# The w_ada products in rows of 16 matmuls of 128 columns, their loads on GpSimd's queue

## The chip, the cores and the metric

One core of one Trainium2 chip runs the whole program. The metric is the device time of one execution in microseconds (us); the runs of the kernel before are given by their median.

## The reference, cut to what matters

Two layers of a decoder trunk over 256 tokens of width 1024, in float32. Each layer is modulated by six vectors of 1024 numbers (shift, scale and gate of the token mixer and of the channel mixer), which come from one conditioning vector `c` and a weight of 24 MB per layer:

```
c_act = silu(c)
for l in range(2):
    mod = c_act @ w_ada[l] + b_ada[l]            # 1024 -> 6 * 1024
    sh1, sc1, g1, sh2, sc2, g2 = split(mod, 6)
    h = rmsnorm(x, ln1_g[l]) * (1 + sc1) + sh1
    x = x + g1 * mixer(h, ...)                   # GLA branch + RWKV-7 branch, gated merge
    h = rmsnorm(x, ln2_g[l]) * (1 + sc2) + sh2
    f = swiglu(h, ...) if l == 0 else moe(h, ...)   # dense on layer 0, top-2 of 8 experts on layer 1
    x = x + g2 * f
return rmsnorm(x, lnf_g)
```

The change is in `c_act @ w_ada[l]` alone. The product has one row, so it has no natural place on a 128x128 array: it is spread over the rest of the program as filler.

## The kernel before, in words

The program runs through `mixer(k, 0)`, `ffn(k, 0)`, `mixer(k, 1)` and `moe(k, 1)`. All weights are streamed from memory. A float32 weight tile `raw` (128x2048, 1 MB, three buffers) is split into a high and a low part, `hi` by ScalarE (L353) and `lo` by VectorE (L354), and `project` (L367) multiplies it in three matmuls of 256 columns per chunk of 128 rows (L379 to L381). In the feed-forward part each of the 22 passes has 48 of these and 24 more in `second` (L1007 to L1009).

**The w_ada work.** The first two groups of layer 0 (shift and scale of the first mixer) are computed at the start, in `start` (L453), from a repacked copy, already in matmuls of 128 columns. The other ten groups (four of layer 0, six of layer 1) are cut into 8 pieces each, 80 pieces in all; a piece is 128 rows by 1024 columns (512 KB), held in a tile `araw` with `ARAW_BUFS = 4` buffers. `feed` (L238) takes the next piece: `c` is the stationary operand, repeated over 32 columns, and four matmuls of 256 columns write to partitions 0 to 31, 32 to 63, 64 to 95 and 96 to 127 of one PSUM bank, so that they use four separate strips of the array. After the eighth piece of a group two more steps are due, one per later call: ScalarE copies the result (L265), and TensorE transposes it (L270) and VectorE adds the bias (L273). A float32 matmul is recorded as two instructions, so a piece is 8 recorded matmuls.

`pace` (L232) decides when `feed` is called: each projection adds its number of 128-row chunks, and a call is made whenever the sum passes `PACE[phase]`, (10, 22, 15) for the mixer of layer 0, the feed-forward part and the mixer of layer 1. `need` (L280) makes the missing calls at once where a modulation vector is used.

`ahead` (L224), called at the end of each `feed`, issues the load of the next piece on SyncE's queue (L229). With four buffers that load goes into the buffer that the feed just before it has read, so it waits until those matmuls are done.

**What sets the order.** In the mixers and the feed-forward part SyncE's queue runs in the order of the program text (`LOADS`, `manual_schedule`); it carries the `raw` loads (L364) and the `araw` loads alike, and what stands behind a waiting load waits too. The order on TensorE, VectorE, ScalarE and GpSimd is made by the framework's scheduler, which plays the program through with estimated times and gives a free engine the earliest ready instruction; an engine then executes that order as it stands. A w_ada piece whose data is there can so be drawn ahead of its place in the text into a hole on TensorE. In `moe` the order is written out by hand, and the queue streams 352 MB of expert weights.

GpSimd does little: it clears tiles at the start, one piece of `TT` in each mixer (L690), and helps at the start and end of `moe` (L1092, L1423, L1436).

Of the kernel before, what the change touches and what calls it, by code (L numbers as in the profile page):

```python
# [9 lines left out]
F32 = mybir.dt.float32  # L10
# [8 lines left out]
P = 128  # L19
T = 256  # L20
D = 1024
KC = 8
# [135 lines left out]
class K:  # L158
# [65 lines left out]
    def ahead(self):  # L224

        while self.todo and len(self.units) < ARAW_BUFS:
            l, g, kc = self.todo.pop(0)
            w = self.st.tile([P, D], F32, name="araw", bufs=ARAW_BUFS)
            self.nc.sync.dma_start(w, self.A["wada"][l, kc * P:(kc + 1) * P, g * D:(g + 1) * D])  # L229
            self.units.append((l, g, kc, w))  # L230

    def pace(self, n):  # L232
        self.paced += n
        if self.paced >= PACE[self.phase]:
            self.paced -= PACE[self.phase]
            self.feed()

    def feed(self):  # L238


        nc = self.nc
        if self.late:
            return self.late.pop(0)()
        if not self.units:
            self.ahead()
        if not self.units:
            return
        l, g, kc, w = self.units.pop(0)
        if kc == 0:
            self.acc = self.ps.tile([P, 512], F32, name="ada")  # L250
        for j in range(4):
            nc.tensor.matmul(self.acc[32 * j:32 * j + 32, :T], self.c32[:, kc, :], w[:, j * T:(j + 1) * T],  # L252
                             start=kc == 0, stop=kc == KC - 1)
        if kc == KC - 1:
            self.late = self.finish(l, g, self.acc)
        self.ahead()
# [141 lines left out]
MOE_BUFS = 15  # L398
PLACES = [f"raw{i}" for i in range(6)] + ["acts", "late"] + [f"raw{i}" for i in range(6, MOE_BUFS)]
FIRST = ["acts", "late"] + [f"raw{i}" for i in (6, 7, 8, 4, 5, 12, 13, 14, 9, 10, 11, 2, 3, 1, 0)] + ["y"]  # L400
PACE = (10, 22, 15)
ARAW_BUFS = 4
SPLIT_BUFS = 5
R_BUFS = 6
# [1315 lines left out]
```

## Time and profile before

| | us |
|---|---|
| median of 3 runs (lowest, highest) | 1825.53 (1822.11, 1826.31) |
| the profiled execution's own time | 1822.8 |
| its span, first to last instruction | 1821.0 |
| TensorE busy | 1749.7 (96%) |
| VectorE busy | 1090.0 (60%) |
| ScalarE busy | 863.9 (47%) |
| GpSimd busy | 15.8 (1%) |

The span and all rows are of the profiled execution. A busy TensorE is not one at its peak. Times in rows count from the span's start. By the trace `start` and the mixer of layer 0 take the first 390 us, the feed-forward part lasts to 608, the mixer of layer 1 to about 945, and the experts take the rest.

### The profile page before, as it was taken

To read this page: it belongs to the slowest core of one execution; us is meant where nothing else is said; L and a number is where in the kernel's file an instruction comes from. 1 tells how busy PE (TensorE), PEld (TensorE's weight loads), DVE (VectorE), ACT (ScalarE), POOL (GpSimd) and SP (SyncE) were. 2 spreads that over 40 slices of the span, in tenths; PEclk is the share of its full clock that TensorE was granted. 3 is DMA by queue.
4 is the path that set the end of the run, shared out by engine and by line. 5 is a ranking of instruction groups with operands and counts; after the bars stand their busy time and mean duration, and the time that the engine had idled before them with its cause. 6 is when DMAs were issued, how large, how long until landed. Compare 5 with 4: busy or idle time off the path is not lost.

```text
span 1821.0 us, 31549 instructions
## 1 busy us (share of the span) xinstructions
PE 1749.7 (96%) x12447; PEld 1409.9 (77%) x12447; DVE 1090.0 (60%) x1876; ACT 863.9 (47%) x1402; POOL 15.8 (1%) x25
## 2 busy tenths in 40 slices
PE   7998999999999999999979999999999999999997
PEld 7787888989898897789977875578756876578754
DVE  3778355665454679566777972289505983189611
ACT  3743243554343564245546761277405772167501
POOL 0000000000000000000010000000000000000001
PEclk9999899999999899899988999999999999999999
DMA  9624166663735432434595989999999999999995
GB/s 347 261 78 178 42 237 239 259 251 117 296 130 218 162 128 93 163 102 177 170 422 213 349 306 412 421 421 421 416 421 421 420 421 417 421 421 421 420 421 216
DMA packets 79981, 521.03 MB, mean 286 GB/s; under 512 B 9520, under 2 KB 10160, under 8 KB 22352
## 3 DMA queue, kind: packets, MB, share of 16 engines
q1 hardware_dynamic: 78672, 517.04, 71.5%
q8 instruction: 100, 1.64, 0.4%
q10 hardware_dynamic: 1152, 1.89, 0.3%
q14 instruction: 57, 0.47, 0.1%
HBM read 517.84 MB, written 1.05 MB: 285 GB/s over the span
## 4 chain that ended last, share of the span: by engine, by line
PE 87%; DVE 7%; DMA 3%; ACT 1%; issue 1%; SPq 0%; ACTq 0%; DVEq 0%
PE pj L1308 11%; PE pj L379 8%; PE pj L381 8%; PE pj L380 8%; PE pj L1312 6%; PE pj L1313 5%; PE pj L1314 5%; PE pc L1327 5%; PE pc L1330 3%; PE pc L1332 3%; PE pc L1331 3%; DMA raw<-win 2%; PE ada L252 2%; PE pg L1357 1%; DVE lo L354 1%; DVE zt L697 1%
## 5 line engine op out<-in xcount | busy, mean ns | idle before, releaser
L1092 DVE TENSOR_TENSOR lo<-raw,hi 128x1024 fp32r<-128x1024 f32 x330 | 396.0, 1222 | 85.2 <-ACT hi L1091 77.4
L1091 ACT ACTIVATE hi<-raw 128x1024 fp32r<-128x1024 f32 x330 | 347.5, 1059 | 128.2 <-PE pj L1313 80.2
L354 DVE TENSOR_TENSOR lo<-raw,hi 128x512 fp32r<-128x512 f32 x402 | 270.3, 689 | 127.6 <-ACT hi L353 119.9
L353 ACT ACTIVATE hi<-raw 128x512 fp32r<-128x512 f32 x402 | 242.4, 627 | 212.1 <-PE pj L380 126.0
L379 PE MATMUL pj<-hh,hi 128*128 128x256 f32 x1040 | 305.5, 294 | 9.3 <-ACT hi L353 6.9
L381 PE MATMUL pj<-hh,lo 128*128 128x256 f32 x1040 | 301.5, 291 | 3.7 <-DVE lo L354 3.5
L380 PE MATMUL pj<-hl,hi 128*128 128x256 f32 x1040 | 298.3, 288 | 0.1
L379 PEld LDWEIGHTS pj<-hh,hi 128*128 128x128 f32 x1040 | 202.4, 195 | 24.9 <-ACT hi L353 13.5
L381 PEld LDWEIGHTS pj<-hh,lo 128*128 128x128 f32 x1040 | 201.7, 194 | 9.8 <-DVE lo L354 7.8
L380 PEld LDWEIGHTS pj<-hl,hi 128*128 128x128 f32 x1040 | 202.3, 195 | 1.8 <-DVE hl L390 0.8
L1308 PE MATMUL pj<-raw,xs 128*64 128x256 f32 x1792 | 201.3, 381 | 0.0
L1312 PE MATMUL pj<-hi,xh 128*128 128x512 f32 x448 | 181.3, 405 | 0.5 <-ACT hi L1091 0.5
L1314 PE MATMUL pj<-lo,xh 128*128 128x512 f32 x448 | 178.4, 398 | 1.9 <-DVE lo L1092 1.9
L1313 PE MATMUL pj<-hi,xl 128*128 128x512 f32 x448 | 177.6, 397 | 0.0
L1308 PEld LDWEIGHTS pj<-raw,xs 128*64 128x64 f32 x1792 | 125.8, 137 | 64.9 <-issue 4.7
L1352 DVE TENSOR_TENSOR late<-late,pj 128x512 f32<-128x512 f32 (+1 forms) x56 | 30.8, 549 | 207.5 <-PE pj L1308 201.0
L1314 PEld LDWEIGHTS pj<-lo,xh 128*128 128x128 f32 x448 | 84.4, 188 | 25.7 <-DVE lo L1092 5.3
L1327 PE MATMUL pc<-raw,as 128*64 128x512 f32 x448 | 102.2, 595 | 0.0
L1312 PEld LDWEIGHTS pj<-hi,xh 128*128 128x128 f32 x448 | 84.6, 189 | 21.4 <-ACT hi L1091 2.0
L1313 PEld LDWEIGHTS pj<-hi,xl 128*128 128x128 f32 x448 | 84.7, 189 | 18.8
L1330 PE MATMUL pc<-hi,acts 128*128 128x512 f32 x224 | 88.2, 394 | 0.0
L1332 PE MATMUL pc<-lo,acts 128*128 128x512 f32 x224 | 87.5, 391 | 0.0
(404 smaller groups left out, 2586.6 us busy)
## 6 DMA issues: line engine op xcount, KB each, us to landing
raw<-moe SPq DMA_DIRECT2D x333, 1024.0 KB, 18.6
raw<-win SPq DMA_DIRECT2D x43, 1024.0 KB, 6.1
araw<-wada SPq DMA_DIRECT2D x80, 512.0 KB, 6.0
raw<-f SPq DMA_DIRECT2D x33, 1024.0 KB, 8.2
raw<-wv SPq DMA_DIRECT2D x8, 1024.0 KB, 5.8
raw<-wog SPq DMA_DIRECT2D x8, 1024.0 KB, 5.8
raw<-wad SPq DMA_DIRECT2D x6, 1024.0 KB, 7.3
raw<-wor SPq DMA_DIRECT2D x4, 1024.0 KB, 5.0
```

Of the source, the lines that this page charges most:

```text
L353: nc.scalar.activation(hi[:, :w], src, AF.Copy)
L354: nc.vector.tensor_tensor(lo[:, :w], src, hi[:, :w].bitcast(F32), ALU.subtract)
L379: nc.tensor.matmul(o, hi[:, s], ah[:, kc, :], start=kc == 0, stop=False)
L380: nc.tensor.matmul(o, hi[:, s], al[:, kc, :], start=False, stop=False)
L381: nc.tensor.matmul(o, lo[:, s], ah[:, kc, :], start=False, stop=kc == nk - 1)
L1091: nc.scalar.activation(hi, w[:, s], AF.Copy)
L1092: eng.tensor_tensor(lo, w[:, s], hi.bitcast(F32), ALU.subtract)
L1308: nc.tensor.matmul(p[64 * n:64 * n + 64, :T], x[:, kc], hi[:, z * 512 + n * T:z * 512 + n * T + T], start=kc == 0, stop=kc == KC - 1)
L1312: nc.tensor.matmul(p, x[0][:, kc], hi[:, s], start=kc == 0, stop=False)
L1313: nc.tensor.matmul(p, x[1][:, kc], hi[:, s], start=False, stop=False)
L1314: nc.tensor.matmul(p, x[0][:, kc], lo[:, s], start=False, stop=kc == KC - 1)
L1327: nc.tensor.matmul(py[0][64 * n:64 * n + 64], act[:, a:a + CAP], hi[:, s], start=first, stop=last)
```

## The change: what it does

A call of `feed` takes two pieces instead of one and issues each as eight matmuls of 128 columns instead of four of 256, so 16 matmuls (32 recorded) stand together. `PACE` is changed to (18, 36, 26), which calls `feed` about half as often. The loads of the pieces are issued on GpSimd's queue instead of SyncE's. Number of pieces, of buffers and of bytes stay as they are.

```diff
@@ ahead
-            self.nc.sync.dma_start(w, self.A["wada"][l, kc * P:(kc + 1) * P, g * D:(g + 1) * D])
+            self.nc.gpsimd.dma_start(w, self.A["wada"][l, kc * P:(kc + 1) * P, g * D:(g + 1) * D])
@@ feed
-        l, g, kc, w = self.units.pop(0)
-        if kc == 0:
-            self.acc = self.ps.tile([P, 512], F32, name="ada")
-        for j in range(4):
-            nc.tensor.matmul(self.acc[32 * j:32 * j + 32, :T], self.c32[:, kc, :], w[:, j * T:(j + 1) * T],
-                             start=kc == 0, stop=kc == KC - 1)
+        for _ in range(2):
+            l, g, kc, w = self.units.pop(0)
+            if kc == 0:
+                self.acc = self.ps.tile([P, 512], F32, name="ada")
+            for h in range(2):
+                for j in range(4):
+                    nc.tensor.matmul(self.acc[32 * j:32 * j + 32, h * P:(h + 1) * P], self.c32[:, kc, :],
+                                     w[:, j * T + h * P:j * T + (h + 1) * P], start=kc == 0 and h == 0,
+                                     stop=kc == KC - 1, skip_group_check=True)
         if kc == KC - 1:
             self.late = self.finish(l, g, self.acc)
         self.ahead()
@@ constants
-PACE = (10, 22, 15)
+PACE = (18, 36, 26)
```

## Rows read from the trace of the kernel before

**Rows 1.** The page: span, and busy time of each engine.
```profile
span 1821.0 us, 31549 instructions
PE 1749.7 (96%) x12447; PEld 1409.9 (77%) x12447; DVE 1090.0 (60%) x1876; ACT 863.9 (47%) x1402; POOL 15.8 (1%) x25
```

**Rows 2.** Window of the experts' stage: PE, PEld, DVE, ACT, POOL busy; clock, DMA, GB/s.
```profile
980.00:1821.00 841.00, 824.59 (x4712) 580.33 (x4712) 479.25 (x546) 412.17 (x514) 5.09 (x11) 1.00 0.97 396
```

**Rows 3.** Waits of SyncE's queue: waiter, releaser, total us, times, longest.
```profile
SPq L229 <- PE ada L252: 460.5, 45, 50.2
```

**Rows 4.** Timeline of SyncE's queue: start of the first load, us to the second's end.
```profile
460.84 9.72 SPq L229 DMA_DIRECT2D araw<-wada  x2
```

**Rows 5.** The chain that ended last, in order of time: start us, us, what.
```profile
302.95 14.27 DMA raw<-win
...
470.66 5.92 DMA raw<-f
...
579.10 5.80 DMA raw<-f
```

**Rows 6.** Windows of the feed-forward part: columns as in the experts' row.
```profile
487.63:496.27 8.64, 8.64 (x75) 8.64 (x73) 4.92 (x9) 4.43 (x8) 0.00 (x0) 1.00 0.96 398
469.53:477.34 7.81, 3.71 (x44) 1.43 (x43) 0.19 (x2) 1.07 (x3) 0.00 (x0) 0.77 0.76 284
477.34:487.63 10.29, 10.29 (x73) 10.07 (x73) 7.24 (x12) 5.83 (x11) 0.00 (x0) 0.85 1.01 419
577.98:585.66 7.68, 3.28 (x43) 1.19 (x42) 0.41 (x3) 1.06 (x3) 0.00 (x0) 0.82 0.79 297
585.66:596.34 10.68, 10.68 (x72) 10.46 (x73) 5.80 (x10) 5.20 (x11) 0.00 (x0) 0.81 1.02 420
390.35:607.86 217.51, 208.87 (x1732) 198.33 (x1733) 112.24 (x196) 100.01 (x188) 0.00 (x0) 0.97 0.55 212
```

**Rows 7.** Timeline of TensorE around three bursts: start us, us, what, xcount.
```profile
533.59 0.28 PE L381 MATMUL pj<-hh,lo 128*128 128x256 f32 x1
533.80 0.64 PE L252 MATMUL ada<-araw,c 128*32 128x256 f32 x8
534.37 0.38 PE L379 MATMUL pj<-hh,hi 128*128 128x256 f32 x1
...
61.57 1.93 PE L252 MATMUL ada<-araw,c 128*32 128x256 f32 x32
...
29.08 0.28 PE L476 MATMUL pj<-hh,lo 128*128 128x256 f32 x1
29.29 1.96 PE L453 MATMUL ada<-raw,c 128*32 128x128 f32 x64
31.18 0.38 PE L473 MATMUL pj<-hh,hi 128*128 128x256 f32 x1
```

**Rows 8.** Windows of line L252 alone: stretch, its length, PE and PEld busy.
```profile
130.00:220.00 90.00, 6.33 (x64) 1.67 (x56) 0.89 0.31 113
...
300.00:390.35 90.35, 10.48 (x142) 3.70 (x131) 1.00 0.66 247
390.35:607.86 217.51, 12.40 (x144) 3.98 (x144) 0.97 0.55 212
...
sum 818.00, PE 56.68 PEld 17.69; mean PE 9.45 PEld 2.95
```

**Rows 9.** Timeline of TensorE in the tail of the first mixer.
```profile
318.01 0.39 PE L379 MATMUL pj<-hh,hi 128*128 128x256 f32 x1 [2.74 <-ACT hi L353]
```

**Rows 10.** Instructions on tile araw: TensorE idle until its loads landed; time to landing.
```profile
  DMA araw<-wada: 8.5, 4
...
DMA to landing us min/median/max: 3.6/6.0/15.6
```

**Rows 11.** Timeline of GpSimd: start us, us, what, idle before and releaser.
```profile
376.98 0.95 POOL L690 MEMSET TT<- 32x1024 f32 x1 [340.54 <-DVE lo L354]
```

## The prediction

> **What bounds the kernel now.** I read the page first, then stages. TensorE is busy 96% of the span and no other engine over 60% [rows 1]; the program is bound by TensorE and by how fast weights reach it. The experts' stage is bound by transfers: the DMA engines are busy 97% of 841 us [rows 2]. It has no w_ada work and its stream begins when the mixer before it gives its buffers back, so what is gained before it moves it forward whole, and nothing is gained inside it. The question is what happens before that stage.
>
> The waits of SyncE's queue give the first answer. In 45 places the queue stood, 460.5 us in all and up to 50.2 us at once, because a w_ada load (L229) waited for the matmuls (L252) that read its buffer [rows 3]. The `raw` loads behind it stand too. Mostly that is covered by three `raw` buffers. In the feed-forward part it is not: a w_ada load issued at 460.84 is followed by another whose issue ends 9.72 us later [rows 4], and only then, at 470.66, comes the next `raw` load, on which the chain that ended last lies for 5.92 us; at 579.10 the same again for 5.80 us [rows 5]. These are the two pile-ups that the reader should see in the windows. A clean pass takes 8.64 us with 72 weight matmuls, 0.12 each. From 469.53 TensorE is busy 3.71 of 7.81 us, and the next pass takes 10.29; from 577.98 it is busy 3.28 of 7.68, and the next takes 10.68 [rows 6]. The longer passes show a granted clock of 0.85 and 0.81: the clock fell to its lower level (1.2 of 2.4 GHz) for part of them, after TensorE had stood half idle. In the holes the scheduler put five w_ada pieces each, ahead of their places, and these too had to wait for their loads.
>
> **The matmuls: rows of 128 columns.** From the matmul before a lone piece to the one after it are 534.37 - 533.59 = 0.78 us; less the ordinary step of 0.12 a piece displaces 0.66 us. Four pieces in one burst last 1.93 us against 0.64 for one [rows 7], so a further piece costs (1.93 - 0.64) / 3 = 0.43, and 0.66 - 0.43 = 0.23 is paid per burst, for going from whole-array matmuls to 32-column ones and back. For 128 columns the start stage has the price: 64 recorded matmuls displace 31.18 - 29.08 - 0.12 = 1.98 us [rows 7]; less 0.23 that is 0.027 each, 0.44 for the 16 of one piece. So the new shape itself gives nothing (0.44 against 0.43), although it doubles matmuls and weight loads; two pieces together give 0.21 us, 1.11 against 2 x 0.66.
>
> What of that is on the path? L252 keeps TensorE busy 56.68 us for 80 pieces [rows 8]. Forty unbroken pairs at 1.09 (2 x 0.44 and the 0.21 by which one burst exceeds its 0.43) are 43.6: the gain is at most 13.1 us. It is at least nothing, if the scheduler cuts pairs into fragments, as it cut some pieces. I count the stretches in which TensorE has no hole to lose the gain in: the feed-forward part, 144 recorded = 9 pairs, 12.40 - 9 x 1.09 = 2.6; and 300 to 390 us, 142 recorded, 10.48 - 8.9 x 1.09 = 0.8 [rows 8]. **3.4 us.** In 130 to 220 us VectorE's triangular inverse leads and the clock stands at 0.89; there, and in the same part of the second mixer, I take nothing: a saved matmul leaves a hole.
>
> **The loads: off SyncE's queue.** `raw` loads then wait for their own buffers alone. In the two pile-ups TensorE loses its idle time, 7.81 - 3.71 = 4.10 and 7.68 - 3.28 = 4.40, and the slow passes after them, 10.29 - 8.64 = 1.65 and 10.68 - 8.64 = 2.04 [rows 6]. Sum **12.2 us**. Bounds: nothing, if the same `raw` loads are late for another reason, and 12.2 with 2.74 more, the hole in the tail of the first mixer [rows 9]. That one I leave out: its `raw` load took 14.27 us from issue to landing [rows 5], so it stood among other transfers and not only behind a wait. I take 12.2 because in the five passes between the pile-ups, where no w_ada load stands in the queue's way, a pass takes 8.64. What is late next in the feed-forward part: nothing; 22 passes of 8.64 are 190 of its 217.5 us.
>
> **GpSimd's queue.** It gets 80 loads that wait for L252. Behind each stands only the next piece and one clearing of `TT`, 0.95 us, done long before `TT` is used; in front of them that clearing can hold them until the tile is free [rows 11]. No load leaves from GpSimd in this trace, so its price is bounded from SyncE's: landing after 3.6 to 15.6 us, median 6.0 [rows 10]. The cover: loads issued after one call are used two calls later, at least 2 x 18 chunks x 3 x 0.12 = 13.0 us in the mixers and 25.9 in the feed-forward part, unless the scheduler draws pieces forward. I take nothing; the upper end is a rival below. One page speaks against this edit: the Trainium skill, SBUF — State Buffer, "SBUF: two separate sides", says that descriptors of a DMA issued from GpSimd can't be written while VectorE runs in a two-port mode, and advises SyncE's or ScalarE's queue. No run here shows it so far.
>
> **PACE.** A group took 10 calls (8 pieces and 2 steps), now 6: in chunks 100 against 108, 220 against 216, 150 against 156. The vectors are ready at nearly the same places, and `need` has nothing to make up before or after. Nothing.
>
> **Sum.** 12.2 + 3.4 = 15.6 us. The profiled execution took 1822.8 (span 1821.0), 2.7 under the median of 1825.5: 1807.2 there, **1809.9** against the median. A measurement can tell 0.2% (3.7 us) of this kernel from no change.
>
> **Rivals.**
> 1. *The pile-ups stay.* The queue was not the cause, or the scheduler's new order makes others. For it: `raw` has only three buffers. Against it: the chain runs from L252 through SyncE to the late load. Only the bursts are left: 1825.5 - 3.4 = 1822.1. The Trainium skill, DMA: Bandwidth & Descriptors, "Issuing engines are not separate DMA queues", says that other issuing engines share the same DMA engines and save only issue time; by that alone this case would hold. What the trace shows is a wait in front of the issue, which that sentence doesn't speak of.
> 2. *Pieces come late on GpSimd's queue: slower.* TensorE executes in order, so a late piece stops it. Four such waits cost 8.5 us before [rows 10], and with the clock a stop costs about 12.2 / 2 = 6.1 us, as the pile-ups did. From three stops on (3 x 6.1 = 18.3 against 15.6) the gain is gone; with one in every second group, five, the time is 1809.9 + 30.5 = 1840.4. It decides if landing exceeds 13.0 us, or where the scheduler draws more than two calls into one hole. For it: the largest landing of 15.6 and the unknown price of that queue; against it: the median of 6.0, and `raw` loads that no longer make holes to draw pieces into.
> 3. *More is gained.* All bursts whole and on the path, and the tail's hole closed: 12.2 + 13.1 + 2.7 = 28.0, 1797.5. Against it: the stretches led by VectorE.
>
> **Chances and range.** Forecast 0.52, rival 1 0.18, rival 2 0.12, rival 3 0.15; 0.03 for a new order that moves a few us otherwise. Rival 1 lies at the edge of no change: 0.11 within it, 0.07 faster. Faster: 0.52 + 0.15 + 0.07 + 0.02 = 0.76; the same 0.11; slower 0.12 + 0.01 = 0.13. The range reaches from rival 3 to a little over rival 1, for its bound of nothing on both terms: 1797 to 1825; it leaves out rival 2 and little else.
>
> **What would show it.** SyncE's waits have no line from L229 to L252, and no w_ada load appears there. The feed-forward part is some 203 us long, with no window in which TensorE is half idle and no pass over 9 us but those that hold a burst. L252 shows 1280 recorded matmuls, in bursts of 32 that last about 1.09 us, busy under 50 us in all. TensorE's idle time before L252 until its loads stays under the 8.5 us of before. The experts' stage is as long as before. Wrong would be: waits of L252 for loads of several us each (rival 2), or `raw` loads on the chain again in the feed-forward part (rival 1).

## The result, and the profile after

The changed kernel took **1805.32 us** (median of 4 runs, 1800.06 to 1807.66) against 1823.82 (4 runs, 1821.64 to 1826.31) for the kernel before: a ratio of 0.9894, 95% interval 0.9865 to 0.9924. The prediction said 1809.9, range 1797 to 1825, faster with 0.76. The profiled execution took 1803.0, 19.8 less than the profiled one of before.

Lines of `feed` and below it move by 2 or 3: L252 is now L254, L353/L354 are L356/L357, L364 is L367, L379 to L381 are L382 to L384. From the page, the span and the engines, which answer to [rows 1]:

```profile
span 1801.2 us, 32937 instructions
PE 1738.4 (97%) x13087; PEld 1423.0 (79%) x13087; DVE 1093.5 (61%) x1876; ACT 872.4 (48%) x1402; POOL 58.2 (3%) x105
```

The windows of the feed-forward part and of the experts' last 841 us (columns as in [rows 2]):

```profile
373.30:580.20 206.90, 203.74 (x1846) 199.54 (x1845) 115.22 (x198) 102.80 (x189) 9.90 (x18) 0.98 0.57 205
...
960.20:1801.20 841.00, 824.72 (x4712) 580.30 (x4712) 478.32 (x546) 411.94 (x513) 5.00 (x11) 1.00 0.97 396
```

In the experts' stage engines, clock and rate are those of before [rows 2], so everything was gained in front of it. Cut at the normalization that opens the feed-forward part (L339, now L342), at the last matmul of that part and at the routing of the experts, the spans divide so:

| | before | after | difference | forecast |
|---|---|---|---|---|
| start and first mixer | 389.0 | 373.3 | -15.7 | -0.8 |
| feed-forward part | 218.7 | 206.9 | -11.8 | -14.8 |
| second mixer | 336.0 | 343.1 | +7.1 | 0 |
| experts | 877.3 | 877.9 | +0.6 | 0 |
| span | 1821.0 | 1801.2 | -19.8 | -15.6 |

The waits of the changed kernel: the w_ada loads now wait on GpSimd, and a `raw` load waits for its own buffer.

```profile
POOL araw L229 <- PE ada L254: 706.7, 46, 79.1
...
SPq L367 <- DVE lo L357: 601.1, 67, 26.4
```

No line from L229 is left on SyncE's queue, where it had 460.5 us [rows 3]. Before, a `raw` load had waited so 34 times only; I read this as the queue mostly reaching it when its buffer had long been free:

```profile
SPq L364 <- DVE lo L354: 197.9, 34, 23.5
```

In the feed-forward part the two pile-ups of [rows 6] are gone. One hole stands at its head: four pieces ran close together just before it, from 369.6 on, ahead of their pace, so the load of the next one left GpSimd only at 370.7 and landed at 376.7. (`need` had nothing to ask for there: the last group of layer 0 was complete at 322.) Further on a pair is whole and takes 1.08 us. Timeline of TensorE after:

```profile
376.72 0.63 PE L254 MATMUL ada<-araw,c 128*32 128x128 f32 x2 [3.16 <-DMA araw<-wada]
...
549.22 1.08 PE L254 MATMUL ada<-araw,c 128*32 128x128 f32 x32
```

### The profile page after: what moved, and what is told of

It is laid out like the page before. It is cut to its first block, busy times and chain, and to the rows that moved or that the text cites. A ratio compares the mean times of both kernels' runs of the same rounds, so it can differ in the third digit from the quotient of the medians.

```text
span 1801.2 us, 32937 instructions
## 1 busy us (share of the span) xinstructions
PE 1738.4 (97%) x13087; PEld 1423.0 (79%) x13087; DVE 1093.5 (61%) x1876; ACT 872.4 (48%) x1402; POOL 58.2 (3%) x105
## 4 chain that ended last, share of the span: by engine, by line
PE 71%; issue 18%; DVE 5%; DMA 4%; ACT 1%; POOL 1%; SPq 0%; POOLq 0%; DVEq 0%; ACTq 0%
PE pj L1311 11%; PE pj L382 6%; PE pc L1330 5%; PE pj L383 5%; PE pj L384 5%; PE pj L1315 5%; PE pj L1317 5%; PE pj L1316 5%; PE pc L1333 3%; PE pc L1335 2%; PE pc L1334 2%; DMA raw<-moe 2%; PE ada L254 1%; PE pg L1360 1%; POOL araw L229 1%
## 5 line engine op out<-in xcount | busy, mean ns | idle before, releaser
L356 ACT ACTIVATE hi<-raw 128x512 fp32r<-128x512 f32 x402 | 252.6, 631 | 291.4 <-PE pj L383 225.9
L357 DVE TENSOR_TENSOR lo<-raw,hi 128x512 fp32r<-128x512 f32 x402 | 275.9, 690 | 172.2 <-ACT hi L356 150.3
L382 PE MATMUL pj<-hh,hi 128*128 128x256 f32 x1040 | 302.9, 292 | 0.1
L384 PE MATMUL pj<-hh,lo 128*128 128x256 f32 x1040 | 297.1, 286 | 0.0
L382 PEld LDWEIGHTS pj<-hh,hi 128*128 128x128 f32 x1040 | 200.0, 193 | 8.9 <-issue 6.9
L384 PEld LDWEIGHTS pj<-hh,lo 128*128 128x128 f32 x1040 | 200.3, 193 | 0.9 <-issue 0.7
L1316 PEld LDWEIGHTS pj<-hi,xl 128*128 128x128 f32 x448 | 84.7, 189 | 18.8
```

What stands on the lines that cost most here:

```text
L356: nc.scalar.activation(hi[:, :w], src, AF.Copy)
L357: nc.vector.tensor_tensor(lo[:, :w], src, hi[:, :w].bitcast(F32), ALU.subtract)
L382: nc.tensor.matmul(o, hi[:, s], ah[:, kc, :], start=kc == 0, stop=False)
L384: nc.tensor.matmul(o, lo[:, s], ah[:, kc, :], start=False, stop=kc == nk - 1)
L1316: nc.tensor.matmul(p, x[1][:, kc], hi[:, s], start=False, stop=False)
```

## The experiments

All kernels are compared with the kernel before on the same chip; its median was 1824 to 1827 in these comparisons. One piece per call goes with `PACE` (10, 22, 15), two with (18, 36, 26), but for E9. The last two columns are from one profiled execution each: the first mixer from the end of its recurrence (the chain of small matmuls that follows VectorE's triangular inverse) to the feed-forward part, and the feed-forward part.

| run | queue of w_ada loads, pieces in flight | per call | columns | us | ratio (95%) | behind the recurrence | feed-forward |
|---|---|---|---|---|---|---|---|
| before | SyncE, 4 | 1 | 256 | | 1 | 174.1 | 218.7 |
| after | GpSimd, 4 | 2 | 128 | 1805.3 | 0.9894 (0.9865 to 0.9924) | 157.6 | 206.9 |
| E1 | GpSimd, 4 | 1 | 256 | 1811.7 | 0.9920 (0.9891 to 0.9948) | 163.3 | 210.7 |
| E2 | SyncE, 4 | 2 | 128 | 1843.8 | 1.0092 (1.0058 to 1.0127) | 173.1 | 219.3 |
| E3 | GpSimd, 4 | 2 | 256 | 1805.8 | 0.9883 (0.9849 to 0.9917) | 159.2 | 205.8 |
| E5 | ScalarE, 4 | 2 | 128 | 1808.7 | 0.9899 (0.9864 to 0.9935) | 158.1 | 205.0 |
| E6 | SyncE, 2 | 1 | 256 | 1812.2 | 0.9920 (0.9904 to 0.9935) | 164.7 | 208.5 |
| E7 | SyncE, 4 | 1 | 128 | 1836.1 | 1.0056 (1.0042 to 1.0070) | 185.7 | 220.9 |
| E8 | as after (same order) | 2 | 128 | 1801.6 | 0.9864 (0.9849 to 0.9878) | 157.6 | 206.8 |
| E9 | as after, other PACE | 2 | 128 | 1807.4 | 0.9886 (0.9863 to 0.9909) | 157.6 | 209.8 |
| E10 | GpSimd, 4 | 1 | 128 | 1806.9 | 0.9902 (0.9879 to 0.9925) | 164.1 | 205.6 |
| E11 | SyncE, 2 | 2 | 128 | 1805.5 | 0.9895 (0.9870 to 0.9920) | 162.6 | 204.5 |
| E12 | SyncE, 4 | 2 | 256 | 1838.3 | 1.0079 (1.0050 to 1.0109) | 173.1 | 222.5 |

**E1 and E2: each half of the change alone.** E1 is the kernel before with one line changed:

```diff
-            self.nc.sync.dma_start(w, self.A["wada"][l, kc * P:(kc + 1) * P, g * D:(g + 1) * D])
+            self.nc.gpsimd.dma_start(w, self.A["wada"][l, kc * P:(kc + 1) * P, g * D:(g + 1) * D])
```

> The kernel before with one edit: the w_ada loads leave from GpSimd's queue; one piece per call, 256 columns, PACE (10, 22, 15). Theory Q (the queue): nearly all the gain is that raw loads no longer stand behind a waiting w_ada load, in the feed-forward part and in the first mixer alike (there the 50 us wait across the recurrence of the first mixer). Then 1807 to 1812, 12 to 17 us below the kernel before; the feed-forward part lasts 205 to 209 us and starts 8 us or more earlier than before. Theory B (the bursts): half as many calls and longer bursts made a better order, and the queue mattered only in the two pile-ups or not at all. Then 1812 to 1822, and the feed-forward part starts within 3 us of before.

E2 is the changed kernel with that line changed back.

> The changed kernel with the w_ada loads back on SyncE's queue: two pieces per call in matmuls of 128 columns, PACE (18, 36, 26). Theory Q: only the bursts are left, 1817 to 1823, 1 to 7 us below the kernel before; waits of SyncE's queue for the w_ada matmuls stay at some hundreds of us, with holes of several us on TensorE where raw loads are late. Theory B: 1806 to 1812, close to the changed kernel.

E1 came out as theory Q said, 14.4 us below the kernel before. Its feed-forward part starts 5.9 us earlier, less than the 8 expected, and is 210.7 long. Its timeline shows why not shorter: both pile-ups are gone, but one late piece holds TensorE, the mechanism of rival 2 at one place.

```profile
387.59 1.08 PE L252 MATMUL ada<-araw,c 128*32 128x256 f32 x6 [4.22 <-DMA araw<-wada]
```

E2 refutes both theories: the rows alone, with their loads on SyncE's queue, are **slower by 17.7 us**. Its waits for w_ada matmuls (sum, times, longest) and the two stretches of the table (its profiled execution, 1851.4, is 7.6 above its median):

```profile
SPq L229 <- PE ada L254: 467.1, 40, 62.7
```

```profile
225.70:398.80 173.10, 164.86 (x1625) 153.55 (x1624) 97.95 (x216) 72.39 (x148) 0.95 (x1) 0.98 0.58 210
398.80:618.10 219.30, 207.23 (x1847) 201.57 (x1846) 113.65 (x198) 101.79 (x189) 0.00 (x0) 0.96 0.53 202
```

TensorE is idle 8.2 and 12.1 us in them (length less busy; 6.4 and 9.8 before), and the longest wait has grown from 50.2 to 62.7. Yet these are not the stretches in which E2 loses against the kernel before: they last 173.1 and 219.3 us against 174.1 and 218.7. In the profiled execution it loses 10.8 us in front of them (225.7 against 214.9) and 18.7 in the second mixer (354.7 against 336.0), and only 6.0 of these 29.5 us are idle TensorE; the rest is busy time. An example is the stretch of the second mixer in front of the inverse, before and, under it, E2:

```profile
630.20:696.30 66.10, 65.65 (x488) 56.83 (x489) 52.17 (x125) 43.84 (x83) 0.00 (x0) 1.00 0.34 118
```

```profile
644.60:716.00 71.40, 69.21 (x513) 61.44 (x513) 52.31 (x124) 44.11 (x84) 0.00 (x0) 0.93 0.34 118
```

The granted clock is 0.93 there, 1.00 before, and over the whole span it was 0.962 to 0.971 in E2's six executions, 0.970 to 0.980 in the twelve of before. Why TensorE was at its lower level more often, no run settles. What E2 does show is that the parts of the change are no terms of a sum: the rows cost time while their loads wait in SyncE's queue, and none once they don't.

**E3, E7, E10, E12: the width.** E3 and E12 take two pieces per call in matmuls of 256 columns, E7 and E10 one piece in matmuls of 128:

```diff
-            for h in range(2):
-                for j in range(4):
-                    nc.tensor.matmul(self.acc[32 * j:32 * j + 32, h * P:(h + 1) * P], self.c32[:, kc, :],
-                                     w[:, j * T + h * P:j * T + (h + 1) * P], start=kc == 0 and h == 0,
-                                     stop=kc == KC - 1, skip_group_check=True)
+            for j in range(4):
+                nc.tensor.matmul(self.acc[32 * j:32 * j + 32, :T], self.c32[:, kc, :], w[:, j * T:(j + 1) * T],
+                                 start=kc == 0, stop=kc == KC - 1)
```

> The changed kernel with each piece as four matmuls of 256 columns, two pieces still together: the width alone. By the prediction's prices (0.44 us for a piece of 128 columns, 0.43 for one of 256) the same within 4 us, 1801 to 1810. The rival is that the width is where the gain lies: then 1812 or more. A pair would show 16 recorded matmuls in some 1.07 us.

> The kernel before with one edit: each piece as eight matmuls of 128 columns, alone, on SyncE's queue, PACE (10, 22, 15). It asks what made the rows alone 17 us slower. If the two pieces of a call did (two loads in a row that wait in front of the raw loads): the same as before within 4 us, 1822 to 1830. If the narrow matmuls did: 1835 or more.

> The kernel before with w_ada loads on GpSimd's queue and each piece as eight matmuls of 128 columns, alone, PACE (10, 22, 15). The narrow matmuls alone cost 10 us with the loads on SyncE's queue. If they are slow in themselves, they cost it here too: about 1821 against the 1811.7 of the same kernel with 256 columns. If it was the pile-ups, which fall elsewhere in a new order (TensorE idle in front of late raw weights and late pieces grew by 14 us there): 1808 to 1816, and no hole in front of a raw weight over 2 us.

> The changed kernel with the loads on SyncE's queue and each piece as four matmuls of 256 columns, two pieces still together. The rows of 128 columns with this queue gave 1843.8, lone pieces of 128 columns 1836.1, lone pieces of 256 columns about 1826. If the width is what costs time with this queue: 1822 to 1832. If the pairs cost it as well: 1833 or more.

With the queue free the width does nothing that can be told: E3 against after 0.9883 and 0.9894, E10 against E1 0.9902 and 0.9920 (E10 lies 1.1 us under its range). A pair takes 1.07 us in E3. With the loads on SyncE's queue E7 is 9 us slower than before. By its own expectation that accuses the narrow matmuls; E10 clears them, and E7's timeline shows the price in new holes in the first mixer, a late piece and then a late `raw` weight (that stretch is 11.6 us longer, with TensorE idle for 15.2 of it against 6.4):

```profile
291.79 0.64 PE L253 MATMUL ada<-araw,c 128*32 128x128 f32 x16 [3.11 <-DMA araw<-wada]
...
327.63 0.58 PE L381 MATMUL pj<-hh,hi 128*128 128x256 f32 x1 [7.65 <-ACT hi L355]
```

E12 has such a hole without narrow matmuls:

```profile
324.09 0.58 PE L380 MATMUL pj<-hh,hi 128*128 128x256 f32 x1 [6.92 <-ACT hi L354]
```

E7 is slow without pairs and E12 without narrow matmuls, so neither is the cause by itself. With waiting loads in SyncE's queue each order of the work has holes of its own, and of the four orders the kernel before is the fastest. That the holes are what sets the four apart is shown for E7 only: in E12, as in E2, the stretch with the hole is 1.0 us shorter than before, and most of the loss lies behind the feed-forward part (22.3 us in its profiled execution, which is 15 us above its median).

**E5, E6, E11: the engine, or the wait?** E5 issues the loads from ScalarE. E6 is the kernel before, E11 is E2, each with

```diff
-        while self.todo and len(self.units) < ARAW_BUFS:
+        while self.todo and len(self.units) < 2:
```

> The changed kernel with the w_ada loads on ScalarE's queue in place of GpSimd's. Theory Q1 (any queue but SyncE's will do): within 4 us of the changed kernel, 1801 to 1810. Theory Q2 (a waiting load stops whatever stands behind it on its engine, and only GpSimd has nothing there): ScalarE's splits hi stand behind loads that wait for L254, TensorE waits for ScalarE, and the time is 1815 to 1850, slower than the changed kernel by 10 us or more.

> The kernel before with one edit: two w_ada pieces in flight in place of four, with the same four buffers, all on SyncE's queue. A load then goes into a buffer that was read two calls earlier, so in the order of the queue the load, and the raw loads behind it, wait for an earlier place. Theory Q (the wait in front of the raw loads is the cause, not the engine that issues): the waits of SyncE's queue for L252 fall from 460 us to under 200, the time falls by 5 to 14 us, 1812 to 1821, less what pieces that come late take back (a piece now has two calls, some 7 us in the mixers, to land). Rival Q3 (the queue of GpSimd or ScalarE brings something else, such as descriptors or DMA rings of its own): the same as before, 1822 to 1830.

> The changed kernel with the loads on SyncE's queue, but two pieces in flight in place of four, so that a load goes into a buffer that the call before the last has read. With four in flight this queue gave 1843.8. Theory Q (where the wait stands in the queue decides): 1803 to 1814, as with GpSimd's queue, less what pieces that come late take (a pair now has one call, some 6.5 us in the mixers, to land). Rival (two pieces in a call are bad for this queue by themselves): 1825 or more.

These settle the cause. On SyncE's own queue two pieces in flight bring the same as GpSimd's queue: E6 0.9920 as E1, E11 0.9895 as the changed kernel, 36 us by the ratios below E2, from which it differs by that one number. A load then goes into a buffer read a call or two earlier. What was wrong in my expectation is the sum of the waits, which I put under 200 us in E6. SyncE's waits in E6 and, under them, in E11:

```profile
SPq L229 <- PE ada L252: 446.1, 65, 42.2
```

```profile
SPq L229 <- PE ada L254: 390.9, 38, 48.3
```

The queue stands almost as long, yet TensorE has no hole over 2 us before a `raw` weight in either. A wait costs only where the `raw` load behind it lands later than TensorE wants it, and in these two runs one call more of lead was enough to prevent that. In both runs no line of L254 or L252 waiting for its own load is left, although a piece has fewer calls to land in.

E5 met theory Q1: ScalarE's queue does as well within the measurement. Where ScalarE's next instruction stood behind such a load, the waits were short, the longest of them:

```profile
ACT t L780 <- PE ada L254: 3.7, 2, 2.3
```

On ScalarE the scheduler places the load among the other work at a time when by its estimate the buffer is free; on SyncE the text places it. That reading is argued from the short waits, not tested by itself. The Trainium skill, DMA: Bandwidth & Descriptors, "Issuing engines are not separate DMA queues", says that transfers run on the same 16 DMA engines whichever engine starts them. The three queues, at 0.989 to 0.990 (SyncE's with two pieces in flight), agree with it.

**E8 and E9: what the second mixer lost.** E8 gives the steps of VectorE's inverse precedence (`with k.tc.high_priority():` around the loop of 30 steps); E9 has another pace:

```diff
-PACE = (18, 36, 26)
+PACE = (18, 28, 26)
```

> The changed kernel with the 30 steps of VectorE's triangular inverse given precedence over other ready work. In the changed kernel 18 splits lo stand between these steps in each mixer, 12 before, at 0.72 us each, and the inverse lasts 5 us longer. If that is what the second mixer lost: the inverse lasts 25 to 32 us in place of 44, and the time falls by 3 to 10 us, 1795 to 1802. Rival: the splits have to be made at some time and TensorE has the work anyway, so that what the inverse gains is lost behind it, as TensorE then stands without split weights: within 4 us of the changed kernel or slower, 1801 to 1815.

> The changed kernel with PACE (18, 28, 26) in place of (18, 36, 26): more w_ada pieces in the feed-forward part, fewer left for the second mixer, whose first stretch took six of them and lasted 26.6 us against 22.5. If a piece costs more there (1.2 us of TensorE at a clock of 0.74) than in the feed-forward part (0.65): 2 to 5 us faster than the changed kernel, 1799 to 1804. Rival: where TensorE is the bound everywhere a piece costs the same at every place: the same within 4 us.

E8 decides nothing: the precedence changed nothing. On every engine and in the queues its instructions stand in the order of the changed kernel, one for one, with the same 18 splits between the steps of the inverse. It is a second measurement of the same program, and a useful one: 0.9864 here and 0.9894 there are 5.5 us apart, so much can two of these comparisons differ without a cause.

E9 met its rival: it moves six pieces from the second mixer to the feed-forward part (22 there, 16 in the changed kernel), that part grows by 2.9 us, and the time is the same within the intervals. Where a piece stands makes no difference that can be told.

## Why the prediction was right, step by step

**The queue in the feed-forward part: right.** 12.2 us were forecast for the two pile-ups. With no hole at its head that part gained 218.7 - 205.6 = 13.1 in E10; E1 gained 8.0, and would have 12.2 without its one late piece of 4.22. The changed kernel has 206.9, with a hole of 3.16 in it; the forecast of some 203 is 206.9 - 3.16 = 203.7. Two pieces fewer in the part (16 in each of these runs, 18 before) are 1.3 of each figure, so the term itself is nearer 11 than 12.2. Rival 1 fell. Rival 2 happened, but once, for 3.16 us, where it needed three stops, and by its second condition: the fifth piece in a row waited, from a third call. (I had also read the 8.5 us in 4 of [rows 10] as four stops: by the same view's list of waiters they are two, told once for the matmul, 3.7, and once for its weight load, 4.7.)

One reading under this term was wrong. I wrote that in the five passes between the pile-ups, at 8.64 us each, no w_ada load stands in the queue's way. In SyncE's timeline before, one did, for 29 us:

```profile
505.00 0.33 SPq L364 DMA_DIRECT2D raw<-f  x1
534.50 0.33 SPq L229 DMA_DIRECT2D araw<-wada  x1
```

The passes stayed at 8.64 because the `raw` loads that they used had been issued in front of it. That the length of a wait is not its price could be read here.

**The bursts: less work for TensorE is shown, the size of the gain is not.** Forecast 3.4 us. With the queue free, pairs have ratios with a mean of 0.9891 (after, E3, E5, E9, E11) and lone pieces of 0.9914 (E1, E6, E10): 0.23%, 4.2 us (5.0 with E8 among the pairs), but the single intervals overlap, and the changed kernel and E8, one program, are 5.5 apart. TensorE's busy time on the pieces is clearer: 58.7 to 62.6 us in the three with lone pieces, 49.8 to 54.2 in the five with pairs. How much of that is on the path stays open. In the changed kernel line L254 is not under 50 us busy, as I wrote: in the second mixer's first stretch the pairs are cut up into bursts of 8 to 16, at a granted clock of 0.74. The line's windows by part, before and after:

```profile
0.00:389.00 389.00, 32.65 (x384) 0.97 0.53 199
389.00:607.70 218.70, 12.40 (x144) 0.97 0.55 213
607.70:630.20 22.50, 1.89 (x16) 0.77 0.30 107
630.20:943.70 313.50, 9.74 (x96) 0.97 0.47 171
```

```profile
0.00:373.30 373.30, 26.97 (x704) 0.98 0.58 213
373.30:580.20 206.90, 10.32 (x256) 0.98 0.57 205
580.20:606.80 26.60, 7.39 (x98) 0.74 0.50 174
606.80:923.30 316.50, 9.51 (x222) 0.97 0.47 169
sum 923.30, PE 54.18; mean PE 13.55
```

**PACE at nothing: wrong in place, right in sum.** I wrote that the vectors are ready at nearly the same places. At 8 and 16 recorded matmuls a piece, 48 pieces stood in the first mixer, 18 in the feed-forward part and 14 in the second mixer; now it is 44, 16 and 20, six of them (two before) in the second mixer's first stretch, which grew from 22.5 to 26.6 us. By E9 that is a shift, not a loss.

**The mixers at nothing: the step that failed.** I counted the queue's waits only in the two pile-ups and wrote "there, and in the same part of the second mixer, I take nothing: a saved matmul leaves a hole". That is an argument about matmuls; it says nothing about loads. The longest wait, 50.2 us, was in my own rows [rows 3], and I didn't look where it stood. SyncE's timeline before:

```profile
164.80 0.37 SPq L364 DMA_DIRECT2D raw<-win  x1
215.41 0.33 SPq L229 DMA_DIRECT2D araw<-wada  x1
```

That wait spans the whole recurrence. Windows of the recurrence and of what follows, before, and under them what follows, after:

```profile
170.90:214.90 44.00, 44.00 (x457) 36.33 (x459) 18.65 (x30) 12.13 (x24) 0.00 (x0) 0.78 0.02 9
214.90:389.00 174.10, 167.75 (x1450) 148.71 (x1444) 100.05 (x221) 74.82 (x153) 0.95 (x1) 1.00 0.59 219
```

```profile
215.70:373.30 157.60, 156.82 (x1607) 148.56 (x1606) 98.06 (x212) 73.61 (x145) 14.36 (x28) 1.00 0.63 228
```

For 44 us the core moved 9 GB/s, and weights beyond those already there began to arrive only at the start of the dense stretch behind. It is not the wait's length that counts, though: E11's 48.3 us stand across the recurrence too, until 222.5, 8 us into that stretch. What differs is how many `raw` loads stand in front of the wait. The loads of `win` issued by the start of the dense stretch, before, after and in E11 (13 in E6 too, 11 in E7, 12 in E2 and E12):

```profile
L364 SPq DMA_DIRECT2D raw<-win x11: 327/373/1057, 32.3 to 164.8; - x11
```

```profile
L367 SPq DMA_DIRECT2D raw<-win x15: 327/328/376, 33.7 to 210.1; - x15
```

```profile
L367 SPq DMA_DIRECT2D raw<-win x13: 328/328/1467, 32.6 to 174.0; - x13
```

TensorE's idle time in the stretch goes with them: 6 to 15 us with 11 or 12 loads, 2.2 and 3.8 with 13, about 1 or less with 15. The dense stretch gained 16.5 us: TensorE's idle time fell from 174.10 - 167.75 = 6.35 to 0.78, 5.6, the tail's hole of 2.74 that I had left out among it; the w_ada work in it from 21.25 to 16.52 us (254 and 448 recorded, 31.8 and 28 pieces), 4.7; and 1450 - 254 = 1196 other matmuls became 1607 - 448 = 1159, 37 fewer, as they were done earlier, at 0.12 each 4.4. The remaining 1.8 I can't assign. The table shows the same with one thing changed at a time: 173 to 186 us where the loads of four pieces in flight wait in SyncE's queue, 163 to 165 for lone pieces without that, 158 to 163 for pairs.

The price is paid in front. More `raw` weights are there, and the scheduler makes more splits `lo` on VectorE between the steps of the inverse; that the one follows from the other I read from the counts, it is not tested by itself. Groups in the inverse of the second mixer, before and after:

```profile
L354 DVE TENSOR_TENSOR lo<-raw,hi 128x512 fp32r<-128x512 f32 x12 | 8.3, 693 | 0.4
```

```profile
L357 DVE TENSOR_TENSOR lo<-raw,hi 128x512 fp32r<-128x512 f32 x18 | 12.5, 693 | 0.6
```

Six more at 0.69 are 4.2 of the 5.2 us by which the inverse grew there (41.1 to 46.3); E7, with 12, has 41.3 there, and E6, with 20, has 49.4. What they save comes back behind the recurrence (78.8 to 74.0). With the moved pieces (+4.1) that leaves 2.6 of the +7.1 of the second mixer, in two stretches that show a lower clock than before (0.97 against 1.00 and 0.81 against 0.84). Of the 4.2 us by which the profiled execution beat the forecast, the first mixer gave 14.9 that I had left out, the second took 7.1, the feed-forward part gained 3.0 less than forecast and the experts took 0.6. That the number came so close is in part luck: a gain that I had not seen and a loss that I had not seen offset each other.

## What to carry to other kernels

In a queue that runs in program order, a load that waits for a buffer holds back every load behind it. Look up where the long waits stand, in every stage, and whether the loads issued in front of each carry TensorE through it; the length of a wait alone does not tell. The cure need not be another engine's queue: loading into a buffer that was read a little earlier did the same here, with half as many pieces in flight.

## What the runs showed of the hardware that was not expected

**The same program at two clocks.** E9 and the changed kernel have the same order on every engine up to the feed-forward part. Yet that part began 8.6 us later in E9's profiled execution. Windows after, then E9, of the stretch to the inverse and of the recurrence:

```profile
54.10:125.00 70.90, 70.43 (x627) 61.18 (x627) 54.15 (x128) 45.39 (x87) 5.28 (x10) 1.00 0.55 193
...
174.40:215.70 41.30, 39.05 (x469) 34.38 (x469) 19.53 (x32) 12.27 (x25) 0.00 (x0) 0.88 0.21 75
```

```profile
54.60:128.70 74.10, 73.57 (x627) 63.24 (x627) 54.23 (x129) 45.59 (x87) 5.28 (x10) 0.95 0.53 184
...
178.60:224.30 45.70, 43.48 (x470) 38.19 (x469) 19.66 (x32) 12.30 (x25) 0.00 (x0) 0.78 0.19 68
...
224.30:381.90 157.60, 156.82 (x1606) 148.58 (x1606) 98.08 (x212) 73.61 (x145) 14.35 (x28) 1.00 0.63 227
```

With the same matmuls the granted clock was 1.00 and 0.95, then 0.88 and 0.78: TensorE was at the lower of its two levels (1.2 of 2.4 GHz) for a longer part in E9, and the two stretches took 3.2 and 4.4 us more. What it did before gives no difference that I can see: in the recurrence both come from the same hole in front of L711, 2.25 and 2.22 us. The dense stretch behind, at a clock of 1.00, is 157.60 both times, and again in E8, where it starts at 216.9 (215.7 and 224.3 in the other two). So in these three profiles of one order the dense stretch compares to 0.1 us, and what lies in front of it only to 8.6 us.

**GpSimd's queue beside a busy VectorE.** The Trainium skill, SBUF — State Buffer, "SBUF: two separate sides", had spoken against this queue. The loads on GpSimd in the changed kernel:

```profile
L229 POOL DMA_DIRECT2D araw<-wada x80: 527/527/720, 2.3 to 792.7; - x80
...
DMA to landing us min/median/max: 4.0/5.7/18.8
```

Issuing one takes 527 ns in the median and 720 at most (328 in the median on SyncE before), it lands after 5.7 us in the median (6.0 before, [rows 10]; the 18.8 is a load of the start, issued at 4.1 us), and a `lo` on VectorE takes 693 ns before and after. No run here shows the cost that the Trainium skill warns of; whether VectorE's instructions were in the mode that it names, no trace tells.
